# Column scales of a delta-rule scan moved to GpSimd in full width, a full-array join, and modulation sums in four column groups

## The chip, the cores and the metric

The kernel runs on one core of one Trainium2 chip. The metric is the device time of one execution in microseconds. The kernel before was timed three times.

## The reference, cut to what matters

One trunk layer over 17 tiles of 128 tokens: one context tile and 16 latent tiles. The part that the change touches is the gated delta rule, which is run over the tiles forwards and backwards, for four heads at a time:

```python
k_beta = k * beta
decay = jnp.where(incl, jnp.exp(jnp.where(incl, diff, 0.0)), 0.0)
a_mat = jnp.where(strict, jnp.einsum('bnhcd,bnhsd->bnhcs', k_beta, k) * decay, 0.0)
rhs = jnp.concatenate([v * beta, k_beta * jnp.exp(g)[..., None]], axis=-1)
sol = lax.linalg.triangular_solve(a_mat + jnp.eye(DN_CHUNK), rhs, lower=True, unit_diagonal=True)
...
v_new = u_c - jnp.einsum('bhck,bhkv->bhcv', w_c, S)
o = jnp.einsum('bhck,bhkv->bhcv', qd, S) + jnp.einsum('bhcs,bhsv->bhcv', qk_c, v_new)
S = S * jnp.exp(gl)[..., None, None] + jnp.einsum('bhck,bhcv->bhkv', kd, v_new)
```

The other part is the modulation, `jax.nn.silu(cond) @ w_mod_l + b_mod_l`, for two conditions (context and latent), 6144 columns wide. Around these stand an input projection, a spatial gating, an output projection and a squared-ReLU MLP.

## The kernel before, in words

The program has three stages. The first (to about 440 us) makes the input projection, the convolution and the products k·k and q·k, writes them to DRAM by tile, and computes the modulation in pieces of 512 columns. The second (about 440 to 1250 us) is the scan, with other matmul work as filler between its steps: the gate and gMLP projections in its first half, the output projection in its second. The third is the MLP.

**Modulation sums** (`mod_steps`). VectorE adds up, for each of the two conditions, `raw * scond` over eight k tiles into an accumulator of 128 partitions by 512 columns. `total` then adds over the partitions: L265 is one matmul a condition with the 128x2 selector `pick` as weights and the 512 columns as the moving operand, into two rows of PSUM. L268 adds the bias, and a DMA writes the row. Seven pieces go this way, five in the first stage and two in the third.

**A unit of the scan** is one tile in one direction, 34 in all. `unit` keeps four heads side by side in tiles of 128x4x128. Its `prep` steps invert a triangular 128x128 matrix for each head, and depend on no other unit. E is made from the row `gb` (g along the free axis, loaded by DMA) and the column table `gcol`: L1020 is |g_col - g_row| head by head on ScalarE, L1021 the exponential, L1023 and L1025 cut out the two triangles on GpSimd (Es and E). L1033 multiplies k·k by beta and Es head by head on VectorE, L1035 puts the ones on the diagonal, L1038, L1039 and L1048 make the f16 forms AH, X and AL. L1045 transposes. Five levels follow (block sizes 2 to 32), each a chain of TensorE (L1065), VectorE (P, L1069), TensorE (L1077 and L1079) and ScalarE (Y, L1080, and X, L1081). The last level, the join of two blocks of 64, is written otherwise: L1095, L1103 and L1105 are matmuls on a quarter of the array (64 partitions in, 64 out), evicted by L1097, L1106 and L1107. A Newton step (L1113, L1114, L1116) and one more product give T, and L1125 scales it by beta/2 head by head on ScalarE.

Its `scan` steps use the state S of the unit before: L1130 scales k by `eglg` (ScalarE, head by head), k·S and L1135 give the right-hand side (VectorE), T times it is evicted as vn (L1143), k·vn and L1155 give the new state `S * egl + ...` (VectorE, head by head), L1157 multiplies q by `eg`, a row broadcast that a DMA loads, and L1166 and L1167 give the output.

**What sets the order.** `at` gives each step a time in units (prep, chain, filler), the steps are emitted by that time, and a list scheduler orders the instructions of each engine. Each engine takes its own in order. GpSimd also has the powers of `rsqrt_cols` (L184).

Of the kernel before, what the change touches and what calls it, by code (L numbers as in the profile page):

```python
# [13 lines left out]
ALU = mybir.AluOpType  # L14
# [49 lines left out]
def hybrid_step(  # L64
# [171 lines left out]
    def mod_steps(jc, pool, stage=None, psum=None, pair=None):  # L236

        u = {}

        def fetch(k):  # L240
            u["raw", k] = raw = stage() if stage else sp.tile([P, 512], F32, tag="raw", name="raw")
            load(out=raw, in_=w_mod[0, k * P : (k + 1) * P, jc * 512 : (jc + 1) * 512])

        def f(k):
            if not pair:
                fetch(k)
            raw = u.pop(("raw", k))
            if k == 0:
                if pair:
                    u["acc"] = pair()  # L250
                else:
                    u["acc"] = [pool.tile([P, 512], F32, tag=f"acc{c}", name="acc", bufs=1) for c in range(2)]
            for c, acc in enumerate(u["acc"]):
                if k == 0:
                    V.tensor_scalar_mul(acc, raw, scond[:, k, c : c + 1])
                else:
                    V.scalar_tensor_tensor(out=acc, in0=raw, scalar=scond[:, k, c : c + 1], in1=acc,
                                           op0=ALU.mult, op1=ALU.add)
            if k == KT - 1 and not pair:
                total()  # L260

        def total():
            ps = (psum or pm1)()
            for c, acc in enumerate(u["acc"]):
                T.matmul(ps[0:2, :], pick[:, c, :], acc, start=c == 0, stop=c == 1)  # L265
# [11 lines left out]
    with ExitStack() as ph:  # L277
# [365 lines left out]
        def decay_steps():  # L643
# [46 lines left out]
            def f3():  # L690
# [7 lines left out]
                V.tensor_scalar_mul(neg2, neg2, -2.0)  # L698
# [247 lines left out]
    with ExitStack() as ph:  # L946
# [34 lines left out]
        pms = {s: f16(f"P{s}") for s in (2, 4, 8, 16, 32)}  # L981
# [3 lines left out]
        def unit(t, d):  # L985

            u = {}
            sg = 1 if d == 0 else -1

# [14 lines left out]
            def scan_loads():  # L1004
# [6 lines left out]
                u["eg"] = load_rows(eg_d, t, d)  # L1011
# [5 lines left out]
            def _():  # L1017
                e = s32("E")
                for h in range(H):
                    A.activation(e[:, h, :], u["gb"][:, h, :], AF.Abs, scale=-1.0, bias=col(gcol, h))  # L1020
                A.activation(e, e, AF.Exp, scale=-1.0)  # L1021
                es = s32("Es")
# [7 lines left out]
            def _():  # L1030
                a = u["KK"]
                for h in range(H):
                    V.scalar_tensor_tensor(out=a[:, h, :], in0=a[:, h, :], scalar=col(beta, h),  # L1033
                                           in1=u["Es"][:, h, :], op0=ALU.mult, op1=ALU.mult)
# [56 lines left out]
            @prep.append  # L1091
            def _():
                p = pd()
                for h in range(H):
                    T.matmul(p[ra, h, 0:64], u["AH"][rb, h, ra], u["Y"][rb, h, rb], start=True, stop=True)  # L1095
                u["P"] = f16("Pm", 1)
                A.activation(u["P"][ra, :, 0:64], p[ra, :, 0:64], AF.Copy, scale=-1.0)  # L1097

            @prep.append
            def _():  # L1100
                py, px = pd(), pd()
                for h in range(H):
                    T.matmul(py[ra, h, 0:64], u["X"][ra, h, ra], u["P"][ra, h, 0:64], start=True, stop=True)  # L1103
                for h in range(H):
                    T.matmul(px[rb, h, 0:64], u["P"][ra, h, 0:64], u["X"][ra, h, ra], start=True, stop=True)  # L1105
                V.tensor_copy(u["Y"][ra, :, rb], py[ra, :, 0:64])  # L1106
                A.copy(u["X"][rb, :, ra], px[rb, :, 0:64])  # L1107
# [12 lines left out]
            def _():  # L1120
# [3 lines left out]
                for h in range(H):  # L1124
                    A.activation(u["T"][:, h, :], p[:, h, :], AF.Copy, scale=col(hbeta, h))  # L1125

            @scan.append
            def _():
                for h in range(H):
                    A.activation(u["kt"][:, h, :], u["kt"][:, h, :], AF.Copy, scale=col(eglg, h))  # L1130
# [8 lines left out]
            def _():  # L1139
                p = pd()  # L1140
# [5 lines left out]
            def _():  # L1146
# [3 lines left out]
                sn = q32("S", 2)  # L1150
                if s is None:
                    A.copy(sn, p)
                else:
                    for h in range(H):
                        V.scalar_tensor_tensor(out=sn[:, h, :], in0=s[:, h, :], scalar=col(egl, h),  # L1155
                                               in1=p[:, h, :], op0=ALU.mult, op1=ALU.add)
                    V.tensor_tensor(out=u["qT"], in0=u["qT"], in1=u["eg"], op=ALU.mult)  # L1157
                u["sn"] = sn
# [19 lines left out]
            u["prep_loads"], u["scan_loads"] = prep_loads, scan_loads  # L1178
# [771 lines left out]
```

## Time and profile before

| | us |
|---|---|
| three timed runs | 2615.22, 2618.3, 2622.74 (median 2618.3) |
| the profiled execution | 2614.33 |
| its span, first to last instruction | 2612.6 |
| TensorE busy over the span | 2572.1 |
| VectorE, ScalarE, GpSimd busy | 1778.0, 1237.3, 229.9 |

The profile names engines by short names: PE is TensorE's matmuls, PEld its weight loads, DVE VectorE, ACT ScalarE, POOL GpSimd. A row of the groups view ends in the busy time and the mean duration, then the time that the engine was idle before these instructions and who ended it. A row of the timeline begins with the start and the length in us. TensorE is pipelined: a matmul's length holds a latency, and what it costs is the distance from its start to the next start.

### The profile page before, as it was taken

To read this page: it belongs to the slowest core of one execution; us is meant where nothing else is said; L and a number is where in the kernel's file an instruction comes from. 1 tells how busy PE (TensorE), PEld (TensorE's weight loads), DVE (VectorE), ACT (ScalarE), POOL (GpSimd) and SP (SyncE) were. 2 spreads that over 40 slices of the span, in tenths; PEclk is the share of its full clock that TensorE was granted. 3 is DMA by queue.
4 is the path that set the end of the run, shared out by engine and by line. 5 is a ranking of instruction groups with operands and counts; after the bars stand their busy time and mean duration, and the time that the engine had idled before them with its cause. 6 is when DMAs were issued, how large, how long until landed. Compare 5 with 4: busy or idle time off the path is not lost.

```text
span 2612.6 us, 44469 instructions
## 1 busy us (share of the span) xinstructions
PE 2572.1 (98%) x15424; PEld 2157.7 (83%) x15424; DVE 1778.0 (68%) x3677; ACT 1237.3 (47%) x3074; POOL 229.9 (9%) x448
## 2 busy tenths in 40 slices
PE   9999999899999999999999999999999999999998
PEld 5999999688888777778888888888888887888887
DVE  5867746766666878885678876666675557775874
ACT  4755555655555757763355543333342432233451
POOL 3112112211111111110000000000000000000000
PEclk9999999899999999999999999999999999999999
DMA  8967637645445657784868789444479979786782
GB/s 282 313 204 221 193 114 243 233 143 174 160 160 170 219 180 265 266 303 155 289 208 260 235 270 313 115 117 121 125 232 376 321 271 318 264 253 214 239 263 89
DMA packets 499751, 580.86 MB, mean 222 GB/s; under 512 B 35692, under 2 KB 298268, under 8 KB 495942
## 3 DMA queue, kind: packets, MB, share of 16 engines
q1 hardware_dynamic: 499526, 578.03, 68.1%
q8 instruction: 121, 1.98, 0.3%
q14 instruction: 104, 0.85, 0.1%
HBM read 398.14 MB, written 179.74 MB: 221 GB/s over the span
## 4 chain that ended last, share of the span: by engine, by line
PE 86%; DMA 6%; DVE 4%; ACT 1%; issue 1%; POOL 0%; SPq 0%; DVEq 0%; POOLq 0%; ACTq 0%
PE f L227 16%; PE f L229 16%; PE f L228 16%; PE pj L227 6%; PE pj L229 6%; PE pj L228 6%; PE pd L995 3%; PE f L1590 2%; PE pm L227 2%; PE pm L229 1%; PE pm L228 1%; DMA raw<-in_w_mod_dram 1%; PE pt L607 1%; PE pd L1166 1%; PE pd L1167 1%
## 5 line engine op out<-in xcount | busy, mean ns | idle before, releaser
L227 PE MATMUL f<-hop,zH 128*128 128x512 f32 x960 | 373.4, 389 | 1.2 <-ACT zH L1476 1.2
L229 PE MATMUL f<-hop,zL 128*128 128x512 f32 x960 | 373.4, 389 | 0.0
L228 PE MATMUL f<-hop,zH 128*128 128x512 f32 x960 | 373.3, 389 | 0.0
L227 PE MATMUL f<-hop,wH 128*128 128x512 f32 x896 | 355.3, 397 | 0.2 <-issue 0.2
L228 PE MATMUL f<-hop,wH 128*128 128x512 f32 x896 | 349.1, 390 | 0.0
L229 PE MATMUL f<-hop,wL 128*128 128x512 f32 x896 | 347.9, 390 | 0.0
L1476 ACT CAST zH<-zraw 128x512 fp32r<-128x512 f32 x240 | 147.1, 620 | 288.1 <-DMA zraw<-s_d 94.4
L227 PEld LDWEIGHTS f<-hop,zH 128*128 128x128 f32 x960 | 180.2, 188 | 39.8 <-ACT zH L1476 1.6
L229 PEld LDWEIGHTS f<-hop,zL 128*128 128x128 f32 x960 | 180.2, 188 | 38.4 <-issue 0.9
L228 PEld LDWEIGHTS f<-hop,zH 128*128 128x128 f32 x960 | 180.2, 188 | 38.3 <-issue 0.9
L1470 DVE TENSOR_TENSOR zL<-zraw,zH 128x512 fp32r<-128x512 f32 x240 | 163.2, 688 | 68.4 <-ACT zH L1476 54.6
L229 PEld LDWEIGHTS f<-hop,wL 128*128 128x128 f32 x896 | 168.2, 188 | 35.2
L227 PEld LDWEIGHTS f<-hop,wH 128*128 128x128 f32 x896 | 168.5, 188 | 33.1 <-issue 0.9
L228 PEld LDWEIGHTS f<-hop,wH 128*128 128x128 f32 x896 | 168.5, 188 | 32.4
L227 PE MATMUL pj<-kH,wH 128*128 128x386 f32 (+2 forms) x568 | 190.4, 338 | 1.7 <-ACT junk L583 1.1
L229 PE MATMUL pj<-kH,wL 128*128 128x386 f32 (+2 forms) x568 | 189.7, 334 | 0.0
L228 PE MATMUL pj<-kL,wH 128*128 128x386 f32 (+2 forms) x568 | 189.0, 334 | 0.0
L184 POOL TENSOR_TENSOR r<-rsq,nhalf 128x1 f32<-128x1 f32 (+1 forms) x38 | 24.2, 637 | 1422.6 <-DVE rsq L183 1422.6
L553 DVE SCALAR_TENSOR_TENSOR cv<-pj,vec,cv 128x384 f32<-128x384 f32 (+2 forms) x164 | 87.1, 539 | 53.3 <-ACT cv L550 51.9
L227 PEld LDWEIGHTS pj<-kH,wH 128*128 128x128 f32 x568 | 107.0, 189 | 7.3 <-issue 4.7
L1476 ACT CAST wH<-s 128x512 fp32r<-128x512 f32 x96 | 59.4, 621 | 105.5 <-DVE s L1470 105.0
L228 PEld LDWEIGHTS pj<-kL,wH 128*128 128x128 f32 x568 | 107.4, 189 | 0.5
(396 smaller groups left out, 5748.0 us busy)
## 6 DMA issues: line engine op xcount, KB each, us to landing
zraw<-z_d SPq DMA_DIRECT2D x212, 256.0 KB
raw<-in_w_ff_dram SPq DMA_DIRECT2D x128, 256.0 KB
hop<-hop_d SPq DMA_DIRECT2D x28, 1024.0 KB
z_d<-c SPq DMA_DIRECT2D x96, 256.0 KB
zraw<-s_d SPq DMA_DIRECT2D x96, 256.0 KB
raw<-in_w_mod_dram SPq DMA_DIRECT2D x80, 256.0 KB
r<-in_w_ff_dram SPq DMA_DIRECT2D x80, 256.0 KB
s_d<-s SPq DMA_DIRECT2D x64, 256.0 KB
```

The lines of the kernel that those rows point to most:

```text
L184: G.tensor_tensor(out=out, in0=t[:np_, :n], in1=nhalf[:np_, :n], op=ALU.pow)
L227: T.matmul(ps, lh, rh, start=first and i == 0, stop=False, skip_group_check=more)
L228: T.matmul(ps, lh, rl, start=False, stop=False, skip_group_check=more)
L229: T.matmul(ps, ll, rh, start=False, stop=last and i == n - 1, skip_group_check=more)
L553: V.scalar_tensor_tensor(out=cv[:, o : o + m], in0=ps[:, s + sh : s + sh + m], scalar=convw[:, w, j : j + 1], in1=cv[:, o : o + m], op0=AL ...
L607: T.matmul(ps[:, i * P : (i + 1) * P], kTt[:, i * P : (i + 1) * P], rhs[:, i * P : (i + 1) * P], start=True, stop=True)
L995: T.matmul(p[:, h, :], lhs[:, h, :], rhs[:, h, :], start=True, stop=True)
L1166: T.matmul(p[:, h, :], u["qT"][:, h, :], s[:, h, :], start=True, stop=False)
L1167: T.matmul(p[:, h, :], u["QK"][:, h, :], u["vn"][:, h, :], start=s is None, stop=True)
L1470: V.tensor_tensor(out=out, in0=a, in1=b, op=op)
L1476: A.copy(h, src)
L1590: T.matmul(ps[:, c : c + P], self.raw[m, kh][:, kp, :], x0[kh][:, kp, :], start=first and kp == 0, stop=last and kp == 3)
```

## The change

- **Scales by GpSimd in full width.** A new helper multiplies (or subtracts) a tile of 128x512 by a table's four columns, each repeated 128 times, on GpSimd: k·k by beta, v by beta/2, k by `eglg`, S by `egl`, and g_row minus g_col. q times `eg` also goes to GpSimd. beta/2 is taken off T and put on v and into `neg2`.
- **Full width elsewhere.** |.| is one ScalarE instruction in place of four, T is one copy in place of four, k·k times Es and the state's sum are one VectorE instruction each in place of four. L1135 stays head by head.
- **Full-array join.** The three products of the join use all 128 partitions in and out, with a P tile (`pms[64]`) that is zero outside its block. The count of matmuls and their 64 columns stay.
- **Sums in column groups.** Each L265 matmul of 512 columns becomes four of 128 columns, whose outputs lie at partitions 0, 32, 64 and 96; L268 becomes four instructions.

```diff
         def total():
             ps = (psum or pm1)()
             for c, acc in enumerate(u["acc"]):
-                T.matmul(ps[0:2, :], pick[:, c, :], acc, start=c == 0, stop=c == 1)
+                for g in range(4):
+                    T.matmul(ps[32 * g : 32 * g + 2, 0:P], pick[:, c, :], acc[:, g * P : (g + 1) * P], start=c == 0,
+                             stop=c == 1)
...
-            V.tensor_tensor(out=row, in0=ps[0:2, :], in1=row, op=ALU.add)
+            for g in range(4):
+                sl = slice(g * P, (g + 1) * P)
+                V.tensor_tensor(out=row[:, sl], in0=ps[32 * g : 32 * g + 2, 0:P], in1=row[:, sl], op=ALU.add)
...
-                V.tensor_scalar_mul(neg2, neg2, -2.0)
+                V.scalar_tensor_tensor(out=neg2, in0=neg2, scalar=-2.0, in1=hbeta, op0=ALU.mult, op1=ALU.mult)
...
+            def times(out, src, tab, op=ALU.mult):
+                cols = tab[:, t, d * 4 : d * 4 + 4].unsqueeze(2).to_broadcast([P, 4, P])
+                G.tensor_tensor(out=out, in0=src, in1=cols, op=op)
...
-                u["eg"] = load_rows(eg_d, t, d)
+                u["eg"] = load_rows(eg_d, t, d) if t else None
+
+            def scale_loads():
+                times(u["vt"], u["vt"], hbeta)
+                times(u["kt"], u["kt"], eglg)
+                if t:
+                    G.tensor_tensor(out=u["qT"], in0=u["qT"], in1=u["eg"], op=ALU.mult)
...
-                for h in range(H):
-                    A.activation(e[:, h, :], u["gb"][:, h, :], AF.Abs, scale=-1.0, bias=col(gcol, h))
+                times(e, u["gb"], gcol, ALU.subtract)
+                A.activation(e, e, AF.Abs)
                 A.activation(e, e, AF.Exp, scale=-1.0)
+                times(u["KK"], u["KK"], beta)
...
-                for h in range(H):
-                    V.scalar_tensor_tensor(out=a[:, h, :], in0=a[:, h, :], scalar=col(beta, h),
-                                           in1=u["Es"][:, h, :], op0=ALU.mult, op1=ALU.mult)
+                V.tensor_tensor(out=a, in0=a, in1=u["Es"], op=ALU.mult)
...
-                    T.matmul(p[ra, h, 0:64], u["AH"][rb, h, ra], u["Y"][rb, h, rb], start=True, stop=True)
-                u["P"] = f16("Pm", 1)
-                A.activation(u["P"][ra, :, 0:64], p[ra, :, 0:64], AF.Copy, scale=-1.0)
+                    T.matmul(p[:, h, 0:64], u["AH"][:, h, :], u["Y"][:, h, rb], start=True, stop=True)
+                A.activation(pms[64][ra, :, rb], p[ra, :, 0:64], AF.Copy, scale=-1.0)
...
-                    T.matmul(py[ra, h, 0:64], u["X"][ra, h, ra], u["P"][ra, h, 0:64], start=True, stop=True)
+                    T.matmul(p[:, h, 0:64], u["X"][:, h, :], pms[64][:, h, rb], start=True, stop=True)
...
-                    T.matmul(px[rb, h, 0:64], u["P"][ra, h, 0:64], u["X"][ra, h, ra], start=True, stop=True)
+                    T.matmul(p[:, h, 64:P], pms[64][:, h, :], u["X"][:, h, ra], start=True, stop=True)
...
-                for h in range(H):
-                    A.activation(u["T"][:, h, :], p[:, h, :], AF.Copy, scale=col(hbeta, h))
+                A.copy(u["T"], p)
...
-                for h in range(H):
-                    A.activation(u["kt"][:, h, :], u["kt"][:, h, :], AF.Copy, scale=col(eglg, h))
...
+                if u["s"] is not None:
+                    times(u["sn"], u["s"], egl)
...
-                    for h in range(H):
-                        V.scalar_tensor_tensor(out=sn[:, h, :], in0=s[:, h, :], scalar=col(egl, h),
-                                               in1=p[:, h, :], op0=ALU.mult, op1=ALU.add)
-                    V.tensor_tensor(out=u["qT"], in0=u["qT"], in1=u["eg"], op=ALU.mult)
+                    V.tensor_tensor(out=sn, in0=sn, in1=p, op=ALU.add)
...
+            at(i - 0.6, u["scale_loads"])
```

TensorE's order in the scan stays almost as it was. In the first stage it moves around the sums. Before, in the third modulation piece (L227 to L229 are projection matmuls, L566 transposes, `pick` the selector):

```order
L227 MATMUL pj<-kH,wH 128x386
L228 MATMUL pj<-kL,wH 128x386
L229 MATMUL pj<-kH,wL 128x386
L265 MATMUL pm<-acc,pick 2x512 x2
L566 MATMUL pt<-ident,x_3230 128x128 x3
```

The same piece now, in two places of the queue with projections between them:

```order
L570 MATMUL pt<-ident,x_2864 128x128 x3
L266 MATMUL pm<-acc,pick 2x128 x3
L600 MATMUL pt<-ident,kn 128x128 x3
L227 MATMUL pj<-kH,wH 128x386
...
L229 MATMUL pj<-kH,wL 128x386
L266 MATMUL pm<-acc,pick 2x128 x3
L570 MATMUL pt<-ident,x_3248 128x128 x3
L266 MATMUL pm<-acc,pick 2x128 x2
```

One burst of two matmuls became eight matmuls in three bursts; of the seven pieces, three are torn like this into two or three bursts and four stay whole.

GpSimd in the middle of the scan, before, for a little over one unit (rs is a power for the filler, Es, E and KK the cuts):

```order
L184 TENSOR_TENSOR rs_6895<-rsq_6896,nhalf_178 128x4
L1023 AFFINE_SELECT Es_7586<-E_7580 128x512
L1025 AFFINE_SELECT E_7580<-E_7580 128x512
L1035 AFFINE_SELECT KK_7429<-KK_7429 128x512
L184 TENSOR_TENSOR rs_7297<-rsq_7298,nhalf_178 128x4
```

And now, one unit's worth:

```order
L997 TENSOR_TENSOR S_8973<-S_8665,egl_195 128x512
L1026 TENSOR_TENSOR qT_8941<-qT_8941,gb_8943 128x512
L1039 AFFINE_SELECT Es_9406<-E_9401 128x512
L1041 AFFINE_SELECT E_9401<-E_9401 128x512
L1049 AFFINE_SELECT KK_9255<-KK_9255 128x512
L997 TENSOR_TENSOR vt_9247<-vt_9247,hbeta_191 128x512
L997 TENSOR_TENSOR KK_9551<-KK_9551,beta_190 128x512
L997 TENSOR_TENSOR kt_9243<-kt_9243,eglg_194 128x512
L997 TENSOR_TENSOR E_9709<-gb_9549,gcol_192 128x512
```

Six instructions of 128x512 with two inputs come to a unit, between the three cuts.

ScalarE at the start of the scan, before, up to the first eviction of a transposed block (Y_6000) and the first level's:

```order
L1038 CAST AH_6115<-KK_6005 128x512
L201 CAST wH_5903<-raw_5901 128x512
L1020 ACTIVATE E_6330<-gb_6181,gcol_192 128x128 x3
L1047 CAST Y_6000<-pd_5995 128x512
L1020 ACTIVATE E_6330<-gb_6181,gcol_192 128x128
L1196 ACTIVATE gw_6035<-pm_5945 128x512
L1130 ACTIVATE kt_6453<-kt_6453,eglg_194 128x128 x4
L1021 ACTIVATE E_6330<-E_6330 128x512
L1080 CAST Y_6000<-pd_6016 128x128x2
```

The same place now:

```order
L1052 CAST AH_6154<-KK_6048 128x512
L1061 CAST Y_6043<-pd_6038 128x512
L1205 ACTIVATE gw_6078<-pm_5992 128x512
L1035 ACTIVATE E_6368<-E_6368 128x512
L1036 ACTIVATE E_6368<-E_6368 128x512
L1094 CAST Y_6043<-pd_6059 128x128x2
```

The four scalings of k and three of the four pieces of E have left the queue ahead of these evictions; the one instruction for |.| that is left reads what GpSimd has subtracted.

More of the change, by code (lines that the diff above doesn't have):

```diff
@@ L980, in hybrid_step @@
         V.tensor_copy(identq, bc4(ident16))
-        pms = {s: f16(f"P{s}") for s in (2, 4, 8, 16, 32)}
+        pms = {s: f16(f"P{s}") for s in (2, 4, 8, 16, 32, 64)}
+        V.memset(pms[64], 0.0)
         two16 = pp.tile([P, P], F16, tag="two16", name="two16")
@@ L1094, in _ @@
                 for h in range(H):
-                    T.matmul(p[ra, h, 0:64], u["AH"][rb, h, ra], u["Y"][rb, h, rb], start=True, stop=True)
-                u["P"] = f16("Pm", 1)
-                A.activation(u["P"][ra, :, 0:64], p[ra, :, 0:64], AF.Copy, scale=-1.0)
+                    T.matmul(p[:, h, 0:64], u["AH"][:, h, :], u["Y"][:, h, rb], start=True, stop=True)
+                A.activation(pms[64][ra, :, rb], p[ra, :, 0:64], AF.Copy, scale=-1.0)
             @prep.append
             def _():
-                py, px = pd(), pd()
+                p = pd()
                 for h in range(H):
-                    T.matmul(py[ra, h, 0:64], u["X"][ra, h, ra], u["P"][ra, h, 0:64], start=True, stop=True)
+                    T.matmul(p[:, h, 0:64], u["X"][:, h, :], pms[64][:, h, rb], start=True, stop=True)
                 for h in range(H):
-                    T.matmul(px[rb, h, 0:64], u["P"][ra, h, 0:64], u["X"][ra, h, ra], start=True, stop=True)
-                V.tensor_copy(u["Y"][ra, :, rb], py[ra, :, 0:64])
-                A.copy(u["X"][rb, :, ra], px[rb, :, 0:64])
+                    T.matmul(p[:, h, 64:P], pms[64][:, h, :], u["X"][:, h, ra], start=True, stop=True)
+                V.tensor_copy(u["Y"][ra, :, rb], p[ra, :, 0:64])
+                A.copy(u["X"][rb, :, ra], p[rb, :, 64:P])
             @prep.append
@@ L1139, in _ @@
             def _():
+                u["sn"] = q32("S", 2)
+                if u["s"] is not None:
+                    times(u["sn"], u["s"], egl)
                 p = pd()
@@ L1149, in _ @@
                 quad(p, u["kt"], u["vn"])
-                sn = q32("S", 2)
+                sn = u["sn"]
                 if s is None:
@@ L1177, in unit @@
             u["prep"], u["scan"] = prep, scan
[L1178 removed]
+            u["prep_loads"], u["scan_loads"], u["scale_loads"] = prep_loads, scan_loads, scale_loads
             return u
```

1 line of the change is left out of this document (removed).

## The prediction

> **What bounds the kernel now.** I read the page first (busy shares and the chain that ended last), then the windows view over the scan, then who ended TensorE's waits there.
>
> ```profile
> span 2612.6 us, 44469 instructions
> PE 2572.1 (98%) x15424; PEld 2157.7 (83%) x15424; DVE 1778.0 (68%) x3677; ACT 1237.3 (47%) x3074; POOL 229.9 (9%) x448
> PE 86%; DMA 6%; DVE 4%; ACT 1%; issue 1%; POOL 0%; SPq 0%; DVEq 0%; POOLq 0%; ACTq 0%
> ```
>
> TensorE has work for 98% of the span, and 86% of the chain runs over it. So time is won where TensorE needs less per matmul, or where it stands still. The windows view has a stretch's length, then the busy time of PE, PEld, DVE, ACT and POOL, and PE's granted clock. These are the start of the scan and its two halves:
>
> ```profile
> 460.00:480.00 20.00, 13.47 (x69) 8.59 (x67) 17.38 (x44) 15.12 (x39) 8.58 (x9) 0.57 0.85 313
> 500.00:860.00 360.00, 356.07 (x3055) 295.39 (x3054) 238.85 (x695) 197.98 (x532) 46.13 (x61) 1.00 0.50 161
> 860.00:1250.00 390.00, 377.11 (x3214) 306.82 (x3213) 292.56 (x741) 251.56 (x762) 57.88 (x69) 1.00 0.71 237
> ```
>
> From 500 to 1250 TensorE is idle for 3.9 + 12.9 = 16.8 us. In the 20 us at the start it idles 6.5 us, and at a mean clock of 0.57 it loses up to 20 x 0.43 = 8.6 us more. So faster eviction engines can bring at most about 32 us. The groups of the scan alone (478 to 1250 us) name the waits:
>
> ```profile
> L1077 PE MATMUL pd<-P,X 128*128 128x64 f16 x668 | 46.7, 194 | 9.5 <-DVE P L1069 8.8 <-ACT o L1170 0.4
> L1065 PE MATMUL pd<-Y,AH 128*128 128x64 f16 x668 | 44.8, 194 | 4.5 <-ACT Y L1080 4.4
> ```
>
> TensorE waits for P from VectorE and for Y from ScalarE, 14.0 us in all; nearly nothing waits for the state.
>
> **The join: full array.** Two stretches of TensorE's timeline in unit 1 and 2 (start, length), and one without a join:
>
> ```profile
> 509.05 0.28 PE L1077 MATMUL pd<-P,X 128*128 128x64 f16 x4
> 509.17 0.28 PE L1079 MATMUL pd<-X,P 128*128 128x64 f16 x4
> 509.38 0.31 PE L1095 MATMUL pd<-Y,AH 64*64 64x64 f16 x4
> 509.62 1.16 PE L995 MATMUL pd<-vn,kt 128*128 128x128 f32 x8
> 510.54 0.48 PE L227 MATMUL pj<-wH,hH 128*128 128x512 f32 x1
> ...
> 512.70 0.29 PE L1065 MATMUL pd<-Y,AH 128*128 128x64 f16 x4
> 512.92 0.21 PE L1103 MATMUL pd<-Pm,X 64*64 64x64 f16 x1
> ...
> 513.05 0.19 PE L1105 MATMUL pd<-X,Pm 64*64 64x64 f16 x1
> 513.17 0.50 PE L227 MATMUL pj<-wH,hH 128*128 128x512 f32 x1
> 513.51 0.40 PE L228 MATMUL pj<-wL,hH 128*128 128x512 f32 x1
> ...
> 523.32 0.48 PE L227 MATMUL pm<-wH,hH 128*128 128x512 f32 x1
> 523.63 0.39 PE L228 MATMUL pm<-wL,hH 128*128 128x512 f32 x1
> ```
>
> Four full-array products of 64 columns cost 0.12 us from start to start (509.05 to 509.17), 0.03 each. Where a 64*64 group follows, the same four cost 0.21 (509.17 to 509.38), and the group itself 0.24: about 0.09 us goes on entering the small form and as much on leaving it. On the full array the two groups would take 0.24 in place of 0.45: 0.21 saved. In the second step L1065 and eight small products take 0.47 (512.70 to 513.17) where twelve full-array ones take 0.36: 0.11 saved, less because the eight overlap in pairs (0.13 for seven steps, 0.019 each). L227 after it costs 0.34 against 0.31 elsewhere: 0.03. That is 0.35 us a unit, and 34 units give **-12 us** on the engine that is the bound (10 if the third part doesn't go). The zeros that the wider product reads cost nothing: 0.03 us is the price of 64 columns on the full array. L1106, L1097 and L1107 keep their shapes.
>
> **Sums in column groups.** One piece in the first stage:
>
> ```profile
> 346.28 1.88 PE L265 MATMUL pm<-acc,pick 128*2 128x512 f32 x4
> 348.09 0.45 PE L227 MATMUL pj<-kH,wH 128*128 128x386 f32 x1
> ```
>
> Two matmuls stand as four instructions of 0.45 us, 1.81 in all. There will be sixteen of 128 columns. Run one by one they cost about 0.115 each (L995, eight in 509.62 to 510.54): 1.84, no gain. Four groups wholly side by side: 0.46, a gain of 1.35. The nearest row for side by side is the join, where products on different parts of the array come out at 0.019 instead of 0.03, or 1.6 to 1. I take pairs: 0.92, a gain of 0.9 a piece and 6.2 for seven. Four additional bursts (the order) each enter and leave the small form, 0.18 us as at the join: 0.7. So **-5.5 us**, between +0.8 and -8.7. Four additions of 2x128 on VectorE in place of one are off the path.
>
> **What leaves ScalarE and VectorE, and what GpSimd gets.**
>
> ```profile
> L1020 ACT ACTIVATE E<-gb,gcol 128x128 f32<-128x128 f32 x136 | 44.0, 393 | 26.6 <-DVE AL L1048 15.7 <-DMA gb<-g_d 10.9
> L1130 ACT ACTIVATE kt<-kt,eglg 128x128 f32<-128x128 f32 x136 | 43.7, 393 | 36.4 <-DMA kt<-kt_d 33.1 <-PE pd L1105 2.9
> L1125 ACT ACTIVATE T<-pd,hbeta 128x128 f32<-128x128 f32 x136 | 38.8, 372 | 4.9 <-PE pd L995 4.6
> L1021 ACT ACTIVATE E<-E 128x512 f32<-128x512 f32 x34 | 21.4, 630 | 0.2
> L1143 ACT COPY vn<-pd 128x512 f32<-128x512 f32 x34 | 19.8, 584 | 36.8 <-PE pd L995 36.7
> L1033 DVE SCALAR_TENSOR_TENSOR KK<-KK,beta,Es 128x128 f32<-128x128 f32 x136 | 44.8, 383 | 4.8 <-POOL Es L1023 2.5 <-DMA KK<-kk_d 2.3
> L1155 DVE SCALAR_TENSOR_TENSOR S<-S,egl,pd 128x128 f32<-128x128 f32 x128 | 35.9, 341 | 13.3 <-PE pd L995 13.3
> L1157 DVE TENSOR_TENSOR qT<-qT,gb 128x512 f32<-128x512 f32 x32 | 22.7, 710 | 25.0 <-DMA qT<-qT_d 24.8
> L1083 DVE TENSOR_TENSOR QK<-QK,E 128x512 f32<-128x512 f32 x34 | 23.4, 688 | 18.7 <-DMA QK<-qk_d 13.6 <-POOL E L1025 5.0
> ```
>
> ScalarE loses 44.0 + 43.7 + 38.8 = 126.5 us and gets one |.| like L1021 (21.4) and one copy like L1143 (19.8) a unit: -85 us. VectorE loses 44.8 + 35.9 + 22.7 = 103.4 and gets 66 instructions like L1083 (0.688): 45.4, so -58 us. None of this is TensorE's time; it counts only through the 14.0 us of waits.
>
> GpSimd gets 200 instructions of 128x512 with two inputs (34 x 4 + 32 x 2). No row has one. The cuts below read one input of that size in 0.64 us, so I take 0.64 to 1.27 (the second input as dear as the first): 128 to 254 us. With the 104 us that it has from 500 to 1250, GpSimd is then busy for a third to a half of the scan. It is also in VectorE's way. Rows with the shortest, median and longest run:
>
> ```profile
> L1035 POOL TENSOR_SCALAR_AFFINE_SELECT KK<-KK x34: 629/639/2832, 456.0 to 1161.7; 128x512 f32<-128x512 f32 x34
> L1243 DVE TENSOR_SCALAR vg<-vg,mv,rs x68: 329/341/789, 477.0 to 901.1; 128x128 f32<-128x128 f32 x68
> L1135 DVE SCALAR_TENSOR_TENSOR vt<-pd,neg,vt x128: 318/342/353, 515.1 to 1234.7; 128x128 f32<-128x128 f32 x128
> ```
>
> L1243 works in SBUF, and its longest run is its median plus 0.45 us; L1135 reads its main input from PSUM and never stretches; a cut once took 2.83 us. So GpSimd and VectorE make each other wait when both work on SBUF. VectorE has some 500 such instructions in 750 us, 0.67 a us. A GpSimd instruction of 0.64 to 1.27 us meets 0.43 to 0.85 of them; each then waits about half its length: 0.12 to 0.36 us an instruction, 24 to 72 us for 200. VectorE ends between -34 and +14 us, about where it was; ScalarE is freer. I put the change of TensorE's waits from 500 on at **0**, between -8 and +20.
>
> The GPSIMD Engine Reference of the Trainium skill (section 3.1) has a two-input addition of 2048 columns at 4497 ns; a quarter is 1.12 us, an estimate inside my range, by which VectorE would get some 60 us of waits back and end level.
>
> **The start of the scan.** The chain view in order of time:
>
> ```profile
> 462.53 2.84 POOL KK L1035
> 466.53 0.89 ACT E L1020 x3
> 467.42 0.47 ACT Y L1047
> 468.67 1.17 ACT kt L1130 x4
> ```
>
> Here everything hangs on ScalarE's queue, and 0.89 + 1.17 us of it goes. But ahead of the cut (KK) GpSimd now has a subtraction, beta times KK and two loads to scale, and ScalarE's |.| waits for GpSimd, with the evictions Y and X queued behind it. I take **-2**, between -6 and +3.
>
> **Sum.** -12 - 5.5 + 0 - 2 = -19.5. A TensorE that is 0.35 us a unit earlier meets the same P and Y somewhat earlier; for that I give back 2.5: -17. The profiled execution took 2614.33 (its span and 1.7 us around it) and would take 2597; it lies 4 us under the median of the runs, 2618.3, from which I get **2601**.
>
> **Rivals.** *(1) The waits shrink as well.* P and Y come earlier, since four short VectorE instructions ahead of P become one and ScalarE is 85 us freer. Of the 14.0 us some 8 go, and at the start 6 in place of 2: 12 us more, 2589. Against it stands GpSimd in VectorE's way.
>
> *(2) The gain is given back.* Sums run one by one (+0.8), and of the join's 12 us eight come back as waits for P, because a level's chain through VectorE and ScalarE, not TensorE, sets the pace of the second half, where 12.9 of the 16.8 us of idle time lie: 2618.3 - 12 + 8 + 0.8 = 2615. Against it: TensorE is busy for 377 of 390 us there.
>
> *(3) Slower: GpSimd holds VectorE up ahead of P.* The place is the second half, VectorE at 292.6 of 390 us (75%). If each of the 200 instructions holds one VectorE instruction for 0.9 us, VectorE gets 180 us, half of them there, and comes to 292.6 - 29 + 90 = 354 of 390 us, 91%. Some 85 of the 167 P's (668 products, four to a P) lie there; at 0.4 us of uncovered delay each TensorE loses 34 us: 2618 - 17 + 34 = 2635. It decides from 0.2 us a P (17 us). For it speaks the 2.83 us cut, against it that filler stands between most levels.
>
> The page "SBUF — State Buffer" of the Trainium skill (section "Who interferes with whom") has this as a lock: of two such instructions the second fully blocks until the first is done. The stretches above agree with it in direction; a whole-length block for each of the 200 would be rival 3.
>
> That the change doesn't do what it says I leave without a chance: no product of the scan is left on a part of the array.
>
> **How the numbers follow.** The forecast has 0.52, rival 1 0.12, rival 2 0.20, rival 3 0.16. About 0.3% (8 us) is what a measurement of this kernel can tell from no change. The forecast's own range is 2592 to 2610, faster; with rival 1 that makes 0.64 faster. Rival 2 is the same, 0.20; rival 3 slower, 0.16. The range of 8 in 10 takes in most of rival 1 and the nearer half of rival 3: 2586 to 2628.
>
> **What would show it.** Right: TensorE's starts around L1109, L1116 and L1118 at 0.03 us with no 0.09 at either side; L266's sixteen in about 0.9 us; VectorE's busy time from 500 to 1250 near 531 us, as the two halves add up before. Wrong: L1083's P late behind stretched KK, QK or x additions, idle time before L1091 (the old L1077) over 20 us (rival 3), or the same total idle time plus the join's gain (rival 2). A two-input GpSimd instruction above 1.3 us would break the bound that I set for it.

## The result and the profile after

| | before | changed |
|---|---|---|
| timed runs, median (lowest to highest) | 2618.85 (2615.22 to 2622.74), six | 2608.19 (2604.09 to 2610.04), six |
| the profiled execution | 2614.33 | 2609.2 |
| its span | 2612.6 | 2607.5 |

The ratio is 0.9954 (95% interval 0.9944 to 0.9964): 10.7 us faster by the medians, 12 by the ratio. The forecast was 2601, the range 2586 to 2628. The profiled execution of before lies below all its timed runs, so the two profiles differ by 5.1 us only. The profiles serve to see where time goes, the ratios to say how much it is. Each ratio in this document is taken against runs of the kernel before made beside it; 0.001 is 2.6 us. From the page of the changed kernel, span, busy shares and chain:

```profile
span 2607.5 us, 44352 instructions
PE 2555.6 (98%) x15508; PEld 2155.5 (83%) x15508; DVE 1768.2 (68%) x3469; ACT 1160.5 (45%) x2734; POOL 459.8 (18%) x648
PE 87%; DVE 5%; DMA 5%; issue 1%; POOL 1%; ACT 1%; SPq 1%; DVEq 0%; POOLq 0%; ACTq 0%
```

TensorE is still the bound, and busy for 16.5 us less. GpSimd's busy time has doubled, ScalarE's fell by 77 us, VectorE's by 10. The windows of the scan (length, then PE, PEld, DVE, ACT, POOL, and PE's clock):

```profile
460.00:480.00 20.00, 15.26 (x106) 11.51 (x106) 15.13 (x31) 10.41 (x24) 13.72 (x14) 0.66 0.55 185
500.00:860.00 360.00, 350.85 (x3029) 291.96 (x3030) 221.96 (x576) 159.27 (x368) 146.24 (x151) 0.99 0.51 161
860.00:1250.00 390.00, 371.51 (x3192) 305.60 (x3191) 290.55 (x635) 216.69 (x605) 165.48 (x159) 0.99 0.71 236
```

From 500 to 1250 TensorE is idle for 9.1 + 18.5 = 27.6 us, where it was 16.8: the engine that got less work waits more. VectorE is busy for 512.5 us, 19 less than before. The join in unit 1, from TensorE's timeline:

```profile
503.92 0.28 PE L1093 MATMUL pd<-X,P 128*128 128x64 f16 x4
504.04 0.28 PE L1109 MATMUL pd<-Y,AH 128*128 128x64 f16 x4
504.15 1.14 PE L1004 MATMUL pd<-vn,kt 128*128 128x128 f32 x8
...
507.20 0.29 PE L1079 MATMUL pd<-Y,AH 128*128 128x64 f16 x4
507.33 0.28 PE L1116 MATMUL pd<-P,X 128*128 128x64 f16 x4
507.44 0.28 PE L1118 MATMUL pd<-X,P 128*128 128x64 f16 x4
507.56 0.48 PE L227 MATMUL pj<-wH,hH 128*128 128x512 f32 x1
507.87 0.40 PE L228 MATMUL pj<-wL,hH 128*128 128x512 f32 x1
```

L1093 and L1109 take 0.23 together (503.92 to 504.15), where it was 0.45; the three groups of the second step take 0.36 (507.20 to 507.56) where it was 0.47; L227 behind them 0.31 in place of 0.34. That is 0.36 us, and the prediction had 0.35. A piece of the modulation sums:

```profile
149.48 0.62 PE L266 MATMUL pm<-acc,pick 128*2 128x128 f32 x16
150.03 0.44 PE L227 MATMUL pj<-kH,wH 128*128 128x386 f32 x1
```

Sixteen products of 128 columns take 0.55 us from start to start, where four of 512 took 1.81. The four groups run wholly side by side: each of the four sets costs 0.14 us, near the 0.115 of one product of 128 columns. The seven pieces, torn ones too, come to 4.86 us by their starts, and came to 12.75.

**Work and waits.** To compare scans I split each distance from one matmul's start to the next. The median distance of the same three forms in a row (the one ahead, this one, the next) counts as work, and what lies over it by more than 25 ns as waiting, time at a lower clock included. The scan runs here from the first projection product of the filler to the last one:

| kernel (one profile each) | ratio to before | 95% interval | scan | work | waits |
|---|---|---|---|---|---|
| before | 1 | | 824.0 | 783.6 | 40.4 |
| sums alone | 0.9971 | 0.9959 to 0.9983 | 827.3 | 783.6 | 43.7 |
| join alone | 0.9967 | 0.9955 to 0.9978 | 824.7 | 769.3 | 55.4 |
| scales alone | 1.0046 | 1.0030 to 1.0062 | 839.2 | 782.2 | 57.0 |
| join + sums | 0.9948 | 0.9932 to 0.9964 | 824.5 | 769.3 | 55.1 |
| changed kernel | 0.9954 | 0.9944 to 0.9964 | 828.2 | 770.0 | 58.1 |
| the same, second time | 0.9957 | 0.9944 to 0.9969 | 822.4 | 769.6 | 52.8 |
| join + sums + scratch products | 1.0042 | 1.0029 to 1.0055 | 843.9 | 768.9 | 75.0 |
| join + sums + scales of preparation | 0.9975 | 0.9964 to 0.9985 | 822.4 | 769.0 | 53.4 |
| join + sums + v, k, q, S | 0.9933 | 0.9921 to 0.9946 | 815.7 | 768.8 | 47.0 |
| the same + subtraction | 0.9982 | 0.9973 to 0.9992 | 827.1 | 769.6 | 57.5 |
| v, k, q, S + kk by beta | 0.9935 | 0.9923 to 0.9948 | 822.2 | 769.8 | 52.5 |
| join + sums + v, k, S | 0.9908 | 0.9894 to 0.9921 | 812.3 | 769.6 | 42.8 |

The work column falls into two levels, 782 to 784 without the join and 769 to 770 with it: the join takes 14 us of work off TensorE in every kernel that has it. What differs beside that are the waits. They scatter by some 5 us between executions of one kernel (58.1 and 52.8), and by 7 between two kernels whose instructions stand in the same order on every engine (47.0 and 54.1, the last experiment). Single rows are read no finer than that.

### The profile page after: what moved, and what is told of

It is laid out like the page before. It is cut to its first block, busy times and chain, and to the rows that moved or that the text cites. A ratio compares the mean times of both kernels' runs of the same rounds, so it can differ in the third digit from the quotient of the medians.

```text
span 2607.5 us, 44352 instructions
## 1 busy us (share of the span) xinstructions
PE 2555.6 (98%) x15508; PEld 2155.5 (83%) x15508; DVE 1768.2 (68%) x3469; ACT 1160.5 (45%) x2734; POOL 459.8 (18%) x648
## 4 chain that ended last, share of the span: by engine, by line
PE 87%; DVE 5%; DMA 5%; issue 1%; POOL 1%; ACT 1%; SPq 1%; DVEq 0%; POOLq 0%; ACTq 0%
PE f L227 16%; PE f L229 16%; PE f L228 16%; PE pj L227 7%; PE pj L229 6%; PE pj L228 6%; PE pd L1004 3%; DMA QK<-qk_d 2%; PE f L1600 2%; PE pm L227 1%; PE pm L228 1%; PE pm L229 1%; PE pt L611 1%; PE pd L1176 1%; PE pd L1175 1%
## 5 line engine op out<-in xcount | busy, mean ns | idle before, releaser
L227 PE MATMUL f<-hop,zH 128*128 128x512 f32 x960 | 373.4, 389 | 1.2 <-ACT zH L1486 1.2
L229 PE MATMUL f<-hop,zL 128*128 128x512 f32 x960 | 373.3, 389 | 0.0
L227 PE MATMUL f<-hop,wH 128*128 128x512 f32 x896 | 355.2, 397 | 0.6 <-DMA hop<-hop_d 0.6
L229 PE MATMUL f<-hop,wL 128*128 128x512 f32 x896 | 347.9, 390 | 0.0
L227 PEld LDWEIGHTS f<-hop,zH 128*128 128x128 f32 x960 | 180.2, 188 | 39.2 <-ACT zH L1486 1.6
L229 PEld LDWEIGHTS f<-hop,zL 128*128 128x128 f32 x960 | 180.2, 188 | 37.8 <-DVE zL L1480 0.4
L229 PEld LDWEIGHTS f<-hop,wL 128*128 128x128 f32 x896 | 168.2, 188 | 35.3
L227 PEld LDWEIGHTS f<-hop,wH 128*128 128x128 f32 x896 | 168.5, 188 | 33.2 <-issue 1.0
L227 PE MATMUL pj<-kH,wH 128*128 128x386 f32 (+2 forms) x568 | 190.6, 338 | 1.7 <-ACT junk L587 1.1
L229 PE MATMUL pj<-kH,wL 128*128 128x386 f32 (+2 forms) x568 | 189.7, 335 | 0.0
L227 PEld LDWEIGHTS pj<-kH,wH 128*128 128x128 f32 x568 | 107.1, 189 | 5.1 <-issue 2.4
L1094 ACT CAST Y<-pd 128x256 f16<-128x256 f32 x170 | 63.7, 375 | 102.2 <-PE pd L1093 101.7
```

Of the source, the lines that this page charges most:

```text
L227: T.matmul(ps, lh, rh, start=first and i == 0, stop=False, skip_group_check=more)
L229: T.matmul(ps, ll, rh, start=False, stop=last and i == n - 1, skip_group_check=more)
L1094: A.copy(y, py)
```

## The experiments

### Which part does what

Theory A: the join's gain stays, and the scales on GpSimd cost time. Theory B: a level's chain through VectorE and ScalarE sets the pace, so that the join's gain comes back as waits, and the scales are neutral.

**Sums alone.** The kernel before with the first two hunks of the diff.

```diff
-                T.matmul(ps[0:2, :], pick[:, c, :], acc, start=c == 0, stop=c == 1)
+                for g in range(4):
+                    T.matmul(ps[32 * g : 32 * g + 2, 0:P], pick[:, c, :], acc[:, g * P : (g + 1) * P], start=c == 0,
+                             stop=c == 1)
```

> The kernel before with the modulation sums in four column groups, and nothing else. In the profile of the changed kernel sixteen matmuls of 128 columns take 0.55 us where four of 512 took 1.81; seven pieces come to 12.75 us before and 4.86 after. Both theories: 7 to 8 us faster than before, none of it in the scan. If it is under 5 us, time that the first stage wins is lost again on the way into the scan.

Measured: 2610.92 (0.9971), 7.6 us faster, as expected. The scan's work is the same as before (783.6). The gain is what the matmuls' rows give (7.9), and nothing of it is lost on the way into the scan.

**Join alone.** The kernel before with `pms[64]` and the three full-array products.

```diff
-                    T.matmul(p[ra, h, 0:64], u["AH"][rb, h, ra], u["Y"][rb, h, rb], start=True, stop=True)
+                    T.matmul(p[:, h, 0:64], u["AH"][:, h, :], u["Y"][:, h, rb], start=True, stop=True)
```

> The kernel before with the full-array join, and nothing else. Theory A (the join's gain stays; the scales on GpSimd cost time): 10 to 12 us faster. Theory B (a level's chain through VectorE and ScalarE sets the pace, so the join's gain comes back as waits for P and Y; the scales are neutral): 2 to 5 us faster, with 7 to 9 us more of TensorE waiting ahead of the products with P and Y.

Measured: 2610.85 (0.9967), 8.6 us faster, between the two theories. TensorE's waits for P, first before, then with the join (us, times, longest):

```profile
PE pd L1077 <- DVE P L1069: 8.8, 14, 1.9
```

```profile
PE pd L1078 <- DVE P L1070: 15.7, 20, 3.6
```

Of 14.3 us of work 8.6 arrive at the end, so 5.7 came back as waits. (The table has 15.0 more of them: the profiled execution of before was faster than the six timed runs above, and that of the join, 2613.98, was the slowest of its kernel.) The waits for P alone grew by 6.9. The pair of sums alone and join + sums shows the same: 6.0 us arrive by the ratios, and waits for P are 11.3 and 13.2. So a part of the gain comes back as waits, 40% or more of it: that much of theory B is shown. Its mechanism, the pace of a level's chain, is not the only one possible. The edit also puts both products of the join's second step into one PSUM tile, and with that ScalarE's eviction of X no longer runs beside VectorE's of Y. In one unit Y's starts at 513.37 before and at 509.54 with the join, and X's, first before, then with the join, at:

```profile
513.38 0.37 ACT L1107 CAST X<-pd 64x256 f16<-64x256 f32 x1 [1.97 <-PE pd L1105]
```

```profile
510.03 0.37 ACT L1107 CAST X<-pd 64x256 f16<-64x256 f32 x1 [2.45 <-DVE Y L1106]
```

X's eviction was released by TensorE and is now released by that of Y. With the join it starts at least 0.44 us after Y's in all 34 units (in the median 1.7 us here and 0.5 in the changed kernel); before, the median is 0. TensorE waits 2.0 us for it in the profile with the join, and not at all in the one before. No run keeps two tiles with the full-array join, so how much of the loss is due to this stays open.

**Scales alone.** All other hunks: the scales on GpSimd and the full-width instructions, join and sums as before.

> The kernel before with the column scales in full width on GpSimd (and |.|, T, kk times Es and the state's sum in full width), without the join and the sums. Theory A: 6 to 12 us slower than before, TensorE waiting longer for P, because VectorE's queue stands behind q.k and kk, which now wait for GpSimd. Theory B: within 3 us of before.

Measured: 2631.23 (1.0046), 12.1 us slower, at the far end of theory A. Although ScalarE and VectorE are rid of all the instructions that the prediction counted off them, TensorE waits 16.6 us more by the table.

**Join and sums, no scales.**

> The kernel before with the full-array join and the sums in column groups; the scales stay head by head on ScalarE and VectorE. Theory A: 18 to 20 us faster than before, so 8 to 10 us faster than the changed kernel. Theory B: 10 to 12 us faster than before, level with the changed kernel.

Measured: 2605.71 (0.9948), 13.6 us faster than before, between the theories. The parts do not add: alone they give -7.6, -8.6 and +12.1, by sum -4.1, and the changed kernel measured -12. With the join in, the scales as a whole move the ratio from 0.9948 to 0.9954 (0.9957 the second time): within the noise. All scales together bring this kernel nothing. Why they cost 12 us without the join and nothing beside it is not shown by any run.

### What of the scales costs

Theory G: GpSimd's reading and writing holds VectorE up, whatever it works on. Theory Q: what costs is that the preparation waits for GpSimd.

**The changed kernel again.**

> The changed kernel once more, on the chip and in the minutes of the next three, as their yardstick. Its six runs lay 0.46% under the kernel before; the kernel before with the join and the sums alone lay 0.52% under it. Again 0.9954, between 0.994 and 0.997.

Measured: 2608.13 (0.9957).

**Scratch products.** Join and sums, all scales as before, and 200 GpSimd products that nobody reads, at the places of the changed kernel's own.

```diff
+            def scratch(n, src):
+                cols = beta[:, t, d * 4 : d * 4 + 4].unsqueeze(2).to_broadcast([P, 4, P])
+                for _ in range(n):
+                    G.tensor_tensor(out=dum, in0=src, in1=cols, op=ALU.mult)
```

> The join and the sums, with all scales as before, and beside them 200 GpSimd products of 128x512 by a table's repeated columns at the places where the changed kernel has its own (three on kT once it has landed, two on gb in the preparation, one on S); their results go to a scratch tile that nothing reads, so they are work added, and the output is the same. Theory G: slower than the kernel with join and sums alone by 8 us or more (as the scales alone cost 12), with VectorE's SBUF instructions stretched. Theory Q: within 3 us of it, since nobody waits for the results.

Measured: 2629.59 (1.0042), 24 us slower than join and sums alone. The busy times of the whole run and the source view of the normalisation (shortest, median, longest), for join and sums:

```profile
PE 2552.5 (98%) x15508; PEld 2153.2 (83%) x15508; DVE 1779.3 (68%) x3699; ACT 1238.0 (48%) x3074; POOL 232.4 (9%) x448
```

```profile
L1247 DVE TENSOR_SCALAR vg<-vg,mv,rs x68: 329/342/790, 467.8 to 888.8; 128x128 f32<-128x128 f32 x68
```

and with the scratch products beside them:

```profile
PE 2557.1 (97%) x15508; PEld 2156.9 (82%) x15508; DVE 1831.0 (70%) x3699; ACT 1239.6 (47%) x3074; POOL 452.5 (17%) x648
```

```profile
L1257 DVE TENSOR_SCALAR vg<-vg,mv,rs x68: 331/345/1200, 474.6 to 906.1; 128x128 f32<-128x128 f32 x68
```

VectorE does the same work, 3699 instructions, and is busy for 51.7 us more, 0.26 us for each of the 200 products; ScalarE's time is nearly the same. Nearly all of the stretch lies in instructions that read SBUF alone: by their lengths summed over the trace, the 68 of the normalisation went from 27.3 to 42.5 us, while the 170 P's, which read their main input from PSUM, took 70.9 and 70.6. So GpSimd beside VectorE has a price of its own, and theory Q alone falls. The 24 us are an upper bound for it: the products also hold the buffers of kT, gb and S, and stand ahead of the cuts in GpSimd's queue. Those shares were not told apart.

**Only the scan's scales** (v, k, q and S on GpSimd) and **only the preparation's** (g_row minus g_col, kk by beta). The first is the changed kernel with

```diff
-                times(e, u["gb"], gcol, ALU.subtract)
-                A.activation(e, e, AF.Abs)
+                for h in range(H):
+                    A.activation(e[:, h, :], u["gb"][:, h, :], AF.Abs, scale=-1.0, bias=col(gcol, h))
...
-                times(u["KK"], u["KK"], beta)
...
-                V.tensor_tensor(out=a, in0=a, in1=u["Es"], op=ALU.mult)
+                for h in range(H):
+                    V.scalar_tensor_tensor(out=a[:, h, :], in0=a[:, h, :], scalar=col(beta, h),
+                                           in1=u["Es"][:, h, :], op0=ALU.mult, op1=ALU.mult)
```

and the second is join and sums with these lines the other way round.

> The changed kernel with the scales of a unit's preparation as before (E from ScalarE head by head, kk times beta and Es head by head on VectorE); v, k, q and S stay with GpSimd. Theory G (GpSimd's reading and writing holds VectorE up, whatever it works on): between the changed kernel and the kernel with join and sums alone, within 2 us of both, since a third of the 200 instructions goes. Theory Q (what costs is that the preparation waits for GpSimd: the subtraction, kk, the cut ahead of P in VectorE's queue): 5 to 10 us faster than the changed kernel, 2598 to 2603.

> The join, the sums, and of the scales only those of the preparation on GpSimd (g_row minus g_col, kk by beta; kk times Es in full width); v, k, q, S and T as before. Theory G: within 2 us of the kernel with join and sums alone (2605.7). Theory Q: slower than that by 4 to 10 us, with longer waits for P.

Measured: 2600.6 (0.9933) and 2611.49 (0.9975). The first beats the changed kernel by 6 us (by the ratios; 7.5 by the medians), the second is 7 slower than join and sums alone. Theory G wanted both level; so the place counts as well as the load. The preparation's scales cost 6 to 7 us. The scan's are worth about 4 (0.9948 to 0.9933), which the intervals do not set apart from nothing. Theory Q had also wanted longer waits for P, and that did not come: the profile with the preparation's scales has 9.5 us of them, that of join and sums alone 13.2, and the scan is no longer (822.4 and 824.5). It is the fastest run of its kernel, and it does not show where the 7 us go.

**The preparation's two parts, one by one**, each beside v, k, q and S: the subtraction (of the last diff the lines on kk alone), and the kk product (the lines on E alone).

> The changed kernel with kk as before (beta and Es on VectorE head by head, no GpSimd product of kk); g_row minus g_col stays with GpSimd. Beside the kernel with the scan's scales alone (2600.6) it adds 34 GpSimd subtractions and takes 102 short instructions off ScalarE. Theory Q1 (the subtraction costs: ScalarE's |.| waits for GpSimd, which waits for the buffer of E): 5 to 8 us slower than 2600.6. Theory Q2 (the kk product costs, since the full-width product with Es now stands in one piece behind GpSimd and ahead of P): within 2 us of 2600.6.

> The changed kernel with E as before (four |.| on ScalarE, no subtraction on GpSimd); kk by beta stays with GpSimd, kk times Es in full width. Theory Q1: within 2 us of 2600.6. Theory Q2: 5 to 8 us slower than 2600.6. If both this and the kernel with the subtraction alone cost 3 to 4 us, it is GpSimd's load as such.

Measured: 2615.58 (0.9982) with the subtraction, 2603.93 (0.9935) with the kk product. It is the subtraction, as theory Q1 said, and it costs more than was expected: 13 us here, 5 to 6 beside the kk product (0.9935 to 0.9954 and 0.9957). TensorE's waits for P with the scan's scales alone, and with the subtraction:

```profile
PE pd L1092 <- DVE P L1084: 12.3, 12, 2.2
```

```profile
PE pd L1092 <- DVE P L1084: 19.7, 22, 2.6
```

But the second kernel with the first one's order (the last experiment) waits 17.2 us for P, so one profile each does not show that the subtraction makes P late. Theory Q1's mechanism is not shown either: ScalarE's |.| waits 20.8 us for GpSimd there, but with the scan's scales alone ScalarE waited about as long (20.6) for VectorE before its own |.|. That the subtraction costs time is shown; how is open.

**q back to VectorE**, v, k and S stay with GpSimd.

```diff
-                if t:
-                    G.tensor_tensor(out=u["qT"], in0=u["qT"], in1=u["eg"], op=ALU.mult)
...
                     V.tensor_tensor(out=sn, in0=sn, in1=p, op=ALU.add)
+                    V.tensor_tensor(out=u["qT"], in0=u["qT"], in1=u["eg"], op=ALU.mult)
```

> The scan's scales without that of q: q times eg goes back to VectorE behind the state's sum, v, k and S stay with GpSimd. If the gain of the scan's scales lies in taking VectorE's wait for the transfer of q (25.0 us in the profile of before) off its queue: 3 to 7 us slower than 2600.6. If VectorE's wait for qk takes its place anyway (34.4 us in the profile with the scan's scales, 9.0 with join and sums alone), then no such loss: within 2 us, or faster by the contention that 32 GpSimd products of 1.29 us no longer make.

Measured: 2595.84 (0.9908), the fastest of all: 23 us under before, 12 under the changed kernel. Two groups of the scan, with q on GpSimd (mean ns of one, then the idle time ahead of it and who ended it):

```profile
L1026 POOL TENSOR_TENSOR qT<-qT,gb 128x512 f32<-128x512 f32 x30 | 39.7, 1325 | 78.2 <-DMA qT<-qT_d 73.7 <-DVE QK L1098 4.4
L1098 DVE TENSOR_TENSOR QK<-QK,E 128x512 f32<-128x512 f32 x31 | 29.8, 961 | 34.4 <-DMA QK<-qk_d 34.4
```

and with q on VectorE:

```profile
L1096 DVE TENSOR_TENSOR QK<-QK,E 128x512 f32<-128x512 f32 x31 | 21.3, 688 | 11.4 <-DMA QK<-qk_d 11.4
L1167 DVE TENSOR_TENSOR qT<-qT,gb 128x512 f32<-128x512 f32 x30 | 20.7, 692 | 24.3 <-DMA qT<-qT_d 24.3
```

VectorE waits 34.4 us for transfers in the one and 11.4 + 24.3 = 35.7 in the other. Taking q off its queue frees nothing, since the next instruction there waits for qk, whose transfer is issued right behind that of q. And because both land together, the product with eg on GpSimd and the one with E on VectorE start together: 0.69 us becomes 0.96 in the mean, ahead of P. TensorE's waits for P are 7.2 us, where they were 12.3 (17.2 in the second kernel of that order):

```profile
PE pd L1090 <- DVE P L1082: 7.2, 8, 1.4
```

The q product also stood 73.7 us at the head of GpSimd's queue, waiting for its transfer, with the cuts behind it. What that cost was not told apart from the stretched product with E.

**q.k times E later.**

```diff
-                    if s == 2:
+                    if s == 8:
```

> The scan's scales on GpSimd, and q.k times E placed behind the level of block size 8, not 2, so that its transfer has longer to land before VectorE comes to it. If P waits because VectorE stands at q.k for its transfer: VectorE's idle time there falls from 34.4 us to under 10, TensorE's waits fall by 4 us or more, 2593 to 2597. Rival: E is held two levels longer, Es of the next unit waits for it on GpSimd, and kk times Es comes later: no gain, or up to 5 us slower.

Measured: 2603.32 (0.9936). The edit did not do what it was meant to: the scheduler put the instruction at the same place in VectorE's queue, and all engines hold the same order as without it. So it tells nothing of P behind q.k. It is a second sample of the same order (0.9936, and 0.9933 without the edit), with waits of 54.1 and 47.0 in the two profiles, and this wait for P where the first had 12.3:

```profile
PE pd L1092 <- DVE P L1084: 17.2, 15, 2.9
```

## Why the prediction was right, and where its sum was not

The direction, the range and the order of the gain were right; 2608 lies midway between the forecast (2601) and the second rival (2615), because parts of both happened. That it came no further from the forecast is in part luck: the join and the sums were taken too low by some 2 us each, which hides some of what the waits took back.

- **The join, -12.** Right in its mechanism and slightly low: 14 us less work in every kernel with it. The two places shown give 0.36 us a unit; the mean over 34 units is 0.42 (14.3 us).
- **The sums, -5.5.** Mis-sized. "I take pairs" was the step: the groups run four abreast, and the pieces lose 7.9 us, near the bound of -8.7 that the prediction had named. The join was the wrong row to read it from, since its small products overlapped in pairs only.
- **GpSimd's price, 0.64 to 1.27 us.** One form lies inside the range, the other just past its upper end. The two forms in the changed kernel:

```profile
L997 POOL TENSOR_TENSOR kt<-kt,eglg x34: 1038/1040/1644, 452.0 to 1207.5; 128x512 f32<-128x512 f32 x34
```

```profile
L1026 POOL TENSOR_TENSOR qT<-qT,gb x32: 1272/1288/1951, 464.2 to 1213.2; 128x512 f32<-128x512 f32 x32
```

  With a table's repeated columns it is 1.04 us in the median, with two full inputs 1.29. The estimate of 1.12 from the Trainium skill's GPSIMD Engine Reference (section 3.1) lies between the two.
- **VectorE, "between -34 and +14".** Right: 19 us less from 500 to 1250, where some 58 were taken off and some 39 came back as longer instructions, 0.2 us for each of the 200 (by the busy time of the whole run, 1778.0 to 1768.2, it is 48 and 0.24); the scratch products measured 0.26. The range under it was worked out loosely: 0.43 to 0.85 instructions that wait for half of 0.64 to 1.27 us make 0.14 to 0.54 us, not 0.12 to 0.36. The measured price lies in both.
- **Waits from 500 on "at 0", with 2.5 given back.** This is the step that failed. -14 for the join and -7.9 for the sums would make 22 us; 10.7 to 12 arrived. So 10 to 11 came back as waits in the scan, where the prediction had put the change of the waits at none and gave back 2.5. The join alone makes 5.7 of it. That is rival 2's effect, which the prediction had set against TensorE's 377 of 390 busy us; a busy share of 97% did not keep the gain from coming back. Whether it came by rival 2's mechanism (P and Y arrive when they arrive, and TensorE meets them sooner) or by the eviction of X behind that of Y is open. The prediction said only that the join's evictions keep their shapes; their times changed.
- **The scales as neutral.** In sum that held (0.9948 and 0.9954), but as a balance of a gain and two costs. v, k and S gain about 10 us (0.9948 to 0.9908), q loses 6.5, the subtraction 5 or more. A part of rival 3 is there: GpSimd holds VectorE up, at up to 24 us where its products take no work off other engines. In the changed kernel, where they do, 1.6 us of loss are left (0.9948 to 0.9954), within the noise.
- **The start of the scan, -2.** It did not come; the sign was the other, and small. The first transposes of X and the first product with R, before:

```profile
L1045 PE MATMUL pd<-ident,X x136: 219/219/330, 459.8 to 1189.5; 128*128 128x128 f16 x136
```

```profile
L995 PE MATMUL pd<-R,X x136: 216/219/230, 498.5 to 1234.4; 128*128 128x128 f16 x136
```

and after:

```profile
L1059 PE MATMUL pd<-ident,X x136: 219/219/330, 452.7 to 1187.9; 128*128 128x128 f16 x136
```

```profile
L1004 PE MATMUL pd<-R,X x136: 219/219/230, 493.2 to 1232.2; 128*128 128x128 f16 x136
```

From 459.8 to 498.5 are 38.7 us, from 452.7 to 493.2 are 40.5. With join and sums alone it is 37.2. The three profiles with all scales have 39.8 to 40.5, the four of kernels without any 36.8 to 38.7. Which of the scales costs there is not shown.

How such a wait looks, at its dearest place in the changed kernel (start, length, and in brackets the idle time ahead):

```profile
719.60 0.40 PE L229 MATMUL pj<-wH,hL 128*128 128x512 f32 x1
719.68 1.28 POOL L1026 TENSOR_TENSOR qT<-qT,gb 128x512 f32<-128x512 f32 x1 [4.91 <-DMA qT<-qT_d]
719.83 0.40 PE L227 MATMUL pj<-wH,hH 128*128 128x512 f32 x1
720.22 1.30 DVE L1097 TENSOR_TENSOR QK<-QK,E 128x512 f32<-128x512 f32 x1 [4.49 <-DMA QK<-qk_d]
721.65 0.63 POOL L1039 TENSOR_SCALAR_AFFINE_SELECT Es<-E 128x512 f32<-128x512 f32 x1 [0.68 <-DVE QK L1097]
722.32 0.69 DVE L1048 TENSOR_TENSOR KK<-KK,Es 128x512 f32<-128x512 f32 x1 [0.80 <-POOL Es L1039]
722.93 0.86 DVE L1206 TENSOR_SCALAR gw<-gw 128x512 f32<-128x512 f32 x1
723.71 0.41 DVE L1083 TENSOR_TENSOR P<-pd,sm 128x256 f16<-128x256 f32 x1
...
724.17 0.37 PE L1091 MATMUL pd<-P,X 128*128 128x64 f16 x4 [3.48 <-DVE P L1083]
...
725.35 0.63 PE L228 MATMUL pj<-wL,hH 128*128 128x512 f32 x1
725.78 0.63 PE L229 MATMUL pj<-wH,hL 128*128 128x512 f32 x1
```

P's input was ready at 718. VectorE stands at q.k for a transfer until 720.22, and then beside GpSimd's q product (1.30 us, not 0.69). The cut Es waits for that, kk for Es, a filler instruction and P come last. TensorE waits 3.48 us, and its matmuls then start 0.43 us apart, where 0.23 is usual (719.60 to 719.83). PE's clock, the third number from the end, stays down up to 730:

```profile
723.00:730.00 7.00, 5.83 (x34) 4.55 (x34) 4.60 (x17) 1.81 (x5) 4.33 (x5) 0.51 0.50 162
```

That loses about 3 us more (half of the six from 724 on). The page "SBUF — State Buffer" of the Trainium skill (section "Who interferes with whom") says that the second of two such instructions is blocked until the first is done. Here GpSimd ends at 720.96 and VectorE 0.56 us later, and q.k alone takes 0.69, which agrees.

## What to carry to other kernels

A saving on an engine that is busy for 97% need not arrive whole: take the work off alone and see how much arrives, before it is booked (here 6 to 9 of 14 us). Look at what else such an edit changes, such as which evictions share a tile. An operation that waits for a transfer is not worth moving to another engine when the next one in the queue waits for the transfer behind it; moved, the two run side by side and hold each other up. Split a change that mixes gains and costs: with only v, k and S on GpSimd this one is worth 23 us in place of 11.

## What the runs showed of the hardware that was not expected

Four column groups of the array, each with its own two output partitions, ran wholly side by side: four f32 products of 128 columns in the time of one (0.55 us for sixteen, against 1.81 for four of 512 columns). A GpSimd product of 128x512 takes 1.04 us when its second input is a table's column repeated by its address pattern, and 1.29 us when it is a full tile. After TensorE's wait of 3.48 us the granted clock was 0.51 from 723 to 730 (the row above), so that the wait cost nearly twice its length at this place. Beside 200 GpSimd products VectorE's busy time grew by 51.7 us, nearly all of it in instructions that read SBUF alone; the P's, which read PSUM, kept their length (70.9 and 70.6 us for 170).
